# Stick-breaking running products: read from PSUM, written to one row of all keys

## The chip, the core and the metric

One core of a Trainium2 chip runs the whole program. A core has five engines that work at the same time, each through its own queue in order: TensorE (PE, matrix products; its weight loads are shown as PEld), VectorE (DVE), ScalarE (ACT), GpSimd (POOL) and SyncE (SP), which issues the DMA transfers. Data lie in SBUF (on-chip memory) or in PSUM (eight banks of 512 float32 columns over 128 partitions, into which TensorE writes its sums). The metric is the device time of one execution in microseconds; the figure given is the median of several runs.

## The reference

Two decoder layers on an input of 2048 positions by 1024 channels, float32. Layer 0 has four forgetting-attention heads ("f") and four stick-breaking heads ("s") of width 128, layer 1 has dilated-window heads. The change touches the stick-breaking heads alone. With z the scaled scores of a query t against the keys s < t:

```python
log_beta = jax.nn.log_sigmoid(z)
log_one_minus = jnp.where(strict, log_beta - z, 0.0)
...
w = jnp.where(strict, jnp.exp(log_beta + later), 0.0)   # later: sum of log_one_minus over the keys after s, before t
outs.append(jnp.einsum('bhqk,bhkd->bhqd', w.astype(v.dtype), v[:, :, :end]))
```

So a weight is sigmoid(z) at its key, times the product of sigmoid(-z) over all later keys of that query: a running product from the last key backwards.

## The kernel before

The program runs in stages: the projection of layer 0 (to about 745 us of the profiled execution), attention of layer 0 (`even_attention`: forgetting heads to about 1003 us, stick-breaking heads to about 1363 us), then layer 1. Every float32 product is made of three passes over high and low halves (`mm3`, lines 91 to 93); a `split` makes the halves, the high one on ACT (line 81), the low one by a subtraction on DVE (line 86).

`even_attention` works in units (kind, head, u): 256 queries, as two blocks i of 128, against all keys up to them. There are 8 units per head and 64 in all. For each block, `qk` goes over the keys in chunks of 512 columns from the last chunk to the first. Per chunk of a stick-breaking head:

- TensorE puts scores into a PSUM bank `ps` (lines 91 to 93; in the last chunk a mask is added, line 733);
- ACT writes sigmoid(-z) to `omb`, a 512-column SBUF buffer out of a ring of four (line 744), and sigmoid(z) into the unit's tile `rows` (line 745);
- DVE scans `omb` backwards in place (line 747): a running product whose start is `carry`, the first column of the scan of the chunk before (that is, of the later keys);
- GpSimd multiplies `rows` with the running product, shifted by one column (line 749, n - 1 columns);
- DVE multiplies the last column of the chunk, whose factor lies in the buffer of the chunk before, with `carry` (line 751, one column).

That is 160 chunks, of which 96 have a `carry`. `pv` then takes the finished `rows` of a unit: TensorE transposes them (line 783), ACT and DVE split them into `pT`, and TensorE multiplies with the values into one bank `po`; DVE multiplies the sum with the gate (line 801). `merged` interleaves `qk` of unit n with `pv` of unit n - 2.

Names and buffers: `k.ps("s")` has four PSUM banks, shared by the scores and `po`; `k.ps("t")` has four more, for the transposes. `k.big` gives one of eight large SBUF slots; during attention each resident head takes two (`kt`, `vt`), the next head's two are taken from u = 4 on, and each unit in flight has one for `rows`. The `res` ring of `k.c2` (four) holds `omb`.

Which instruction stands where in an engine's queue is decided when the program is built: a planner places the instructions by the order of the program text and an estimate of their durations, gives them slots, and adds the waits that data and slots need.

Of the kernel before, what the change touches and what calls it, by code (L numbers as in the profile page):

```python
# [11 lines left out]
AF = mybir.ActivationFunctionType  # L12
OP = mybir.AluOpType
# [4 lines left out]
P = 128  # L18
S = 2048
D = 1024  # L20
KT = D // P
CH = 512
# [14 lines left out]
class K:  # L37
# [28 lines left out]
    def c2(self, shape=(P, CH), dt=F32, name="c2", tag="c"):  # L66

        return self.cs.tile(list(shape), dt, name=name, tag=tag, bufs={"c": 4, "res": 4}.get(tag, 2))
# [608 lines left out]
def merged(*gens):  # L677

    live = [[g, n, 0] for g, n in gens]
    while live:  # L680
        live.sort(key=lambda e: (e[2] + 0.5) / e[1])
        e = live[0]
        if next(e[0], "end") == "end":
            live.remove(e)
        e[2] += 1
# [3 lines left out]
def even_attention(k, tail):  # L689
    tc, nc = k.tc, k.nc  # L690
    c2 = k.c2
    scale = float(P) ** -0.5
    heads, bias = {}, {}

    def load_head(kind, h):
        T, V = (k.fT, k.v["f"]) if kind == "f" else (k.sT, k.v["s"])
        kt = k.big([P, 4, 2, CH], F32R, name="kt")
        vt = k.big([P, 4, 2, TPC, P], F32R, name="vt")

        def chunk(c):  # L700
            s = slice(c * CH, (c + 1) * CH)
            nc.sync.dma_start(kt[:, c].bitcast(F32), T["k"][:, h, :, s].bitcast(F32))
            for z in range(2):
                nc.sync.dma_start(vt[:, c, z].bitcast(F32),
                                  V[s, z, h * P:(h + 1) * P].rearrange("(j p) d -> p j d", p=P).bitcast(F32))

        heads[kind, h] = kt, vt
        return chunk

    def load_q(kind, h, u):  # L710
        T = k.fT if kind == "f" else k.sT
        if kind == "f" and u % 2 == 0:
            c = u // 2
            bias[h, c] = c2(name="bias")
            nc.sync.dma_start(bias[h, c], k.ncum[h:h + 1, c * CH:(c + 1) * CH].to_broadcast([P, CH]))
        q = c2([P, 2, 2 * P], F32R, name="qT", tag="q")
        nc.sync.dma_start(q.bitcast(F32), T["q"][:, h, :, u * 2 * P:(u + 1) * 2 * P].bitcast(F32))
        return q

    def qk(kind, h, u, q, tile):  # L720
        kt, vt = heads[kind, h]
        c = u // 2
        for i in range(2):
            rows = tile[:, i]
            a = [q[:, z, i * P:(i + 1) * P] for z in range(2)]
            nk = (u * 2 + i + 1) * P
            carry = None
            for kc in range(c, -1, -1):
                n = CH if kc < c else nk - c * CH
                ps = k.ps("s")  # L730
                k.mm3(ps[:, :n], a, [kt[:, kc, z, :n] for z in range(2)], True, kc < c)
                if kc == c:
                    nc.tensor.matmul(ps[:, n - P:n], k.identb, k.after if kind == "f" else k.notbefore,
                                     start=False, stop=True)
                dst = rows[:, kc * CH:kc * CH + n]
                if kind == "f":
                    m = k.small.tile([P, 1], F32, name="m")
                    nc.vector.tensor_tensor_reduce(
                        out=dst, in0=ps[:, :n], in1=bias[h, kc][:, :n], op0=OP.add, op1=OP.max,
                        scale=1.0, scalar=3.0 * NEG if carry is None else carry, accum_out=m)  # L740
                    carry = m
                else:
                    o = c2(name="omb", tag="res")
                    nc.scalar.activation(o[:, :n], ps[:, :n], AF.Sigmoid, scale=-scale)  # L744
                    nc.scalar.activation(dst, ps[:, :n], AF.Sigmoid, scale=scale)
                    oo = o[:, :n]
                    nc.vector.tensor_tensor_scan(oo[:, ::-1], oo[:, ::-1], oo[:, ::-1],  # L747
                                                 1.0 if carry is None else carry, OP.mult, OP.bypass)
                    nc.gpsimd.tensor_tensor(dst[:, :n - 1], dst[:, :n - 1], o[:, 1:n], op=OP.mult)  # L749
                    if carry is not None:  # L750
                        nc.vector.tensor_tensor(dst[:, n - 1:n], dst[:, n - 1:n], carry, op=OP.mult)  # L751
                    carry = o[:, 0:1]
                yield
            if kind == "f":
                nm = k.small.tile([P, 1], F32, name="nm")
                nc.vector.tensor_scalar(nm, carry, -1.0, None, op0=OP.mult)
                den = k.small.tile([P, 2], F32, name="den")
                cuts = [(b, min(b + 2 * CH, nk)) for b in range(0, nk, 2 * CH)]
                for z, (b, e) in enumerate(cuts):
                    nc.scalar.activation(rows[:, b:e], rows[:, b:e], AF.Exp, bias=nm,  # L760
                                         accum_out=den[:, z:z + 1])
                if len(cuts) == 2:
                    nc.vector.tensor_tensor(den[:, :1], den[:, :1], den[:, 1:], op=OP.add)
                rd = k.small.tile([P, 1], F32, name="rd")
                nc.vector.reciprocal(rd, den[:, :1])
                for b, e in cuts:
                    nc.gpsimd.tensor_scalar(rows[:, b:e], rows[:, b:e], rd, 1.0, op0=OP.mult, op1=OP.mult)

    def pv(kind, h, u, rows):

        vt = heads[kind, h][1]
        po = k.ps("s")
        gt = c2([P, 2 * P], name="gate", tag="pT")
        m = (0 if kind == "f" else 4) + h
        cols = slice(u * 2 * P, (u + 1) * 2 * P)
        nc.sync.dma_start(gt, k.gT[:, m, cols])

        def transposed(jj):
            pt = k.ps("t")
            hl = k.wps.tile([P, 2, 2, 2 * P], F32R, name="pT", tag="wp")  # L780
            for jx in range(2):
                for i in range(jx if jj == u else 0, 2):
                    nc.tensor.transpose(pt[:, (jx * 2 + i) * P:(jx * 2 + i + 1) * P],  # L783
                                        rows[:, i, (jj * 2 + jx) * P:(jj * 2 + jx + 1) * P], k.ident)
            flat = [hl[:, z].rearrange("p j t -> p (j t)") for z in range(2)]
            for s in (slice(0, 2 * P), slice(3 * P, 4 * P)) if jj == u else (slice(0, 4 * P),):
                k.split(flat[0][:, s], flat[1][:, s], pt[:, s])
            return hl

        ready = transposed(0)  # L790
        for jj in range(u + 1):
            yield
            hl = ready
            if jj < u:
                ready = transposed(jj + 1)
            for jx in range(2):
                j = jj * 2 + jx
                i0 = P if jj == u and jx else 0
                a = [vt[:, j // TPC, z, j % TPC] for z in range(2)]
                k.mm3(po[:, i0:2 * P], a, [hl[:, z, jx, i0:] for z in range(2)], j == 0, j == 2 * u + 1)  # L800
        nc.vector.tensor_tensor(gt, po[:, :2 * P], gt, op=OP.mult)
        nc.sync.dma_start(k.mixT[:, m, cols], gt)
# [4 lines left out]
    def slopes(g, hf):  # L807

        t = k.w4([P, HG, 2, P], name="slopes")
        for h in range(HG):  # L810
            slope = 2.0 ** (-8.0 * (g * HEADS + hf * HG + h + 1) / (3 * HEADS))
            nc.gpsimd.tensor_scalar(t[:, h], k.dist, -slope32(slope) * GROUPS[g][1], 1.0, op0=OP.mult, op1=OP.mult)
        nc.sync.dma_start(k.bias[g, hf], t)
# [6 lines left out]
    q = load_q(*units[0])  # L820
# [2 lines left out]
    past = []  # L823
    for n, (kind, h, u) in enumerate(units):
        rows = k.big([P, 2, S], name="rows")
        gens = [(qk(kind, h, u, q, rows), 2 * (u // 2 + 1))]
        if n + 1 < len(units):
            q = load_q(*units[n + 1])
        nxt = order.index((kind, h)) + 1
        if u == 1 and nxt <= 6:  # L830
            slopes((nxt - 1) // 2, (nxt - 1) % 2)
        if nxt < len(order) and u >= 3:
            if u == 3:
                chunk = load_head(*order[nxt])
            else:
                chunk(u - 4)
        if len(past) == 2:
            v = past.pop(0)
            gens.append((pv(*v[0], v[1]), v[0][2] + 1))
        merged(*gens)  # L840
        past.append(((kind, h, u), rows))
# [389 lines left out]
```

## Time and profile before

| | |
|---|---|
| median of 3 runs | 2896.94 us (2895.7 to 2902.72) |
| the profiled execution | 2898.2 us, its span 2896.1 us |
| TensorE, weight loads | 93%, 85% of the span busy |
| VectorE | 73% |
| ScalarE | 57% |
| GpSimd | 44% |
| mean granted TensorE clock | 0.975 of full speed |

The profile is a record of one execution. A group of instructions is shown as: line, engine, operation, output<-inputs, shape, xcount | busy us, mean ns of one | idle time of the engine just before them and what ended it. A row of waits is: who waited <- for whom: us in total, times, longest. A row of the timeline is: start in us, duration in us, engine, line, operation. Busy shares in the slices are tenths (9 is 90% or more), 40 slices over the span, each 72.4 us.

### The profile page before, as it was taken

How to read it: one execution, taken by the hardware profiler on the slowest of the kernel's cores; microseconds unless marked ns; L12 is line 12 of the kernel's file. 1: busy time of each engine (PE TensorE's matmuls, PEld its weight loads, DVE VectorE, ACT ScalarE, POOL GpSimd, SP SyncE). 2: the span in 40 equal slices, each digit the busy share in tenths (PEclk: the TensorE clock that was granted, in tenths of full speed). 3: DMA queues.
4: the chain of work that ended last, by engine and by line, in shares of the span. 5: the costliest groups of instructions: out<-in, count | busy, mean ns of one | idle time of the engine just before them, and what ended most of it. 6: DMA issues, size and time to landing. Idle time of an engine off the chain costs nothing.

```text
span 2896.1 us, 56017 instructions
## 1 busy us (share of the span) xinstructions
PE 2693.4 (93%) x20191; PEld 2467.0 (85%) x20191; DVE 2107.1 (73%) x4480; ACT 1650.2 (57%) x3992; POOL 1281.4 (44%) x996
## 2 busy tenths in 40 slices
PE   4999999999999988887887999999989999999998
PEld 3899878998899877776887999999978999999876
DVE  7747785675677799999976966666687586663866
ACT  5446453465566666665455564555565477765642
POOL 5545365434233355555654745343335442422322
PEclk8999999999999999998998999999999999999999
DMA  3556635545544433312567463424533445444665
GB/s 117 168 170 224 197 125 170 168 129 185 159 152 135 137 106 116 110 48 75 177 204 228 147 215 99 145 94 148 163 123 98 139 147 161 139 139 138 217 233 197
DMA packets 388164, 437.39 MB, mean 151 GB/s; under 512 B 31472, under 2 KB 319536, under 8 KB 387888
## 3 DMA queue, kind: packets, MB, share of 16 engines
q1 hardware_dynamic: 387888, 433.83, 46.4%
q8 instruction: 159, 2.61, 0.4%
q14 instruction: 117, 0.96, 0.1%
HBM read 279.16 MB, written 154.57 MB: 150 GB/s over the span
## 4 chain that ended last, share of the span: by engine, by line
PE 61%; DVE 24%; DMA 5%; issue 4%; ACT 4%; POOL 1%; SPq 1%; DVEq 0%; ACTq 0%; POOLq 0%
PE ps L91 16%; PE ps L92 16%; PE ps L93 16%; DVE omb L747 4%; PE ps L783 3%; DVE A L86 2%; DVE wop L86 2%; PE ps L1035 2%; DVE S L86 2%; PE ps L1025 2%; PE ps L1006 2%; PE ps L951 1%; DVE lp L319 1%; DVE pT L86 1%; DVE c L277 1%
## 5 line engine op out<-in xcount | busy, mean ns | idle before, releaser
L210 POOL TENSOR_TENSOR wraw<-wraw 128x512 f32<-128x512 f32 (+1 forms) x320 | 444.4, 1396 | 486.5 <-DVE wop L86 210.8
L81 ACT ACTIVATE wop<-wraw 128x512 fp32r<-128x512 f32 (+1 forms) x560 | 350.6, 630 | 372.0 <-PE ps L93 302.1
L86 POOL TENSOR_TENSOR wop<-wraw,wop 128x512 fp32r<-128x512 f32 (+1 forms) x240 | 328.7, 1372 | 508.7 <-ACT wop L81 490.4
L91 PE MATMUL ps<-wop,S 128*128 128x256 f32 (+1 forms) x1792 | 518.9, 290 | 20.0 <-DVE c L277 10.2
L92 PE MATMUL ps<-wop,S 128*128 128x256 f32 (+1 forms) x1792 | 514.2, 287 | 12.2 <-DVE wop L86 9.4
L92 PE MATMUL ps<-wop,A 128*128 128x256 f32 (+1 forms) x1792 | 512.4, 286 | 6.2 <-DVE wop L86 6.0
L91 PE MATMUL ps<-wop,A 128*128 128x256 f32 (+1 forms) x1792 | 511.8, 286 | 6.8 <-ACT u L282 3.1
L93 PE MATMUL ps<-wop,S 128*128 128x256 f32 (+1 forms) x1792 | 514.8, 288 | 0.0
L93 PE MATMUL ps<-wop,A 128*128 128x256 f32 (+1 forms) x1792 | 509.7, 285 | 0.0
L86 DVE TENSOR_TENSOR wop<-wraw,wop 128x512 fp32r<-128x512 f32 (+1 forms) x320 | 266.8, 835 | 236.1 <-ACT wop L81 234.8
L91 PEld LDWEIGHTS ps<-wop,S 128*128 128x128 f32 x1792 | 343.6, 192 | 25.6 <-ACT wop L81 9.6
L92 PEld LDWEIGHTS ps<-wop,S 128*128 128x128 f32 x1792 | 344.4, 192 | 15.4 <-DVE wop L86 10.3
L91 PEld LDWEIGHTS ps<-wop,A 128*128 128x128 f32 x1792 | 341.8, 191 | 11.3 <-issue 4.0
L92 PEld LDWEIGHTS ps<-wop,A 128*128 128x128 f32 x1792 | 342.5, 191 | 8.7 <-DVE wop L86 7.6
L93 PEld LDWEIGHTS ps<-wop,S 128*128 128x128 f32 x1792 | 344.4, 192 | 3.6 <-issue 2.9
L93 PEld LDWEIGHTS ps<-wop,A 128*128 128x128 f32 x1792 | 342.6, 191 | 1.4 <-issue 0.9
L749 POOL TENSOR_TENSOR rows<-rows,omb 128x511 f32<-128x511 f32 (+3 forms) x160 | 189.9, 1198 | 162.4 <-DVE rows L751 76.5
L81 ACT ACTIVATE pT<-ps 128x512 fp32r<-128x512 f32 (+2 forms) x352 | 166.9, 508 | 137.0 <-PE ps L783 69.2
L277 DVE TENSOR_TENSOR c<-u,ps 128x512 f32<-128x512 f32 (+1 forms) x254 | 165.2, 657 | 98.3 <-PE ps L93 86.6
L747 DVE TENSOR_TENSOR_SCAN omb<-omb 128x512 f32<-128x512 f32 (+3 forms) x160 | 220.0, 1379 | 5.9 <-ACT omb L744 3.4
L86 DVE TENSOR_TENSOR pT<-ps,pT 128x512 fp32r<-128x512 f32 (+2 forms) x352 | 189.3, 560 | 31.2 <-ACT pT L81 30.0
L92 PE MATMUL ps<-pT,vt 128*128 128x256 f32 (+1 forms) x576 | 182.2, 317 | 30.7 <-DVE pT L86 30.5
(216 smaller groups left out, 6619.3 us busy)
## 6 DMA issues: line engine op xcount, KB each, us to landing
wraw<-in_odd_w_in_dram SPq DMA_DIRECT2D x80, 512.0 KB, 3.9
wraw<-in_even_w_in_dram SPq DMA_DIRECT2D x64, 512.0 KB, 4.4
ld<-qk SPq DMA_DIRECT2D x106, 256.0 KB, 3.1
qk<-c SPq DMA_DIRECT2D x96, 256.0 KB, 2.4
lp<-hT SPq DMA_DIRECT2D x60, 256.0 KB, 3.4
uu<-ot SPq DMA_DIRECT2D x96, 132.0 KB, 2.0
fin<-uu SPq DMA_DIRECT2D x16, 792.0 KB, 4.8
hT<-te SPq DMA_DIRECT2D x48, 256.0 KB, 3.9
```

Source lines behind the costliest of these rows:

```text
L81: nc.scalar.activation(hi, src, AF.Copy)
L86: (nc.vector if lo_on == "dve" else nc.gpsimd).tensor_tensor(lo, src, hi.bitcast(F32), op=OP.subtract)
L91: mm(out, a[0], b[0], start=start, stop=False, skip_group_check=more)
L92: mm(out, a[0], b[1], start=False, stop=False, skip_group_check=more)
L93: mm(out, a[1], b[0], start=False, stop=stop, skip_group_check=more)
L210: tt = lambda e, o, x, y, op, s: e.tensor_tensor(o[:, s], x[:, s], y[:, s], op=op)
L277: nc.vector.tensor_tensor(out[g], x[g], y[g], op=OP.add)
L747: nc.vector.tensor_tensor_scan(oo[:, ::-1], oo[:, ::-1], oo[:, ::-1], 1.0 if carry is None else carry, OP.mult, OP.bypass)
L749: nc.gpsimd.tensor_tensor(dst[:, :n - 1], dst[:, :n - 1], o[:, 1:n], op=OP.mult)
L783: nc.tensor.transpose(pt[:, (jx * 2 + i) * P:(jx * 2 + i + 1) * P], rows[:, i, (jj * 2 + jx) * P:(jj * 2 + jx + 1) * P], k.ident)
L1006: nc.tensor.matmul(scores(hp, e), q[pr, za, hp], ring[pr, zb, hp, blocks], start=i == 0, stop=i == 2)
L1025: nc.tensor.transpose(pp[:, i * P:(i + 1) * P], row[:, h // 2, h % 2, b], k.ident)
```

## The change

In `qk`, for stick-breaking heads: each unit gets a second large slot, `rest`, of the same shape as `rows`, passed as `left`. ACT writes sigmoid(z) to `rows` first and then sigmoid(-z) over the scores in their PSUM bank. The scan reads that bank backwards and writes to the columns of the chunk in `rest`; its second operand, which the operation bypasses, is one column of the identity matrix, repeated. Since the running products of all chunks now lie side by side, the GpSimd product of a chunk with a later neighbour covers all n columns, the shifted operand reaching one column into that neighbour, and the one-column product on DVE is gone. The buffer `omb` is gone too.

```diff
-    def qk(kind, h, u, q, tile):
+    def qk(kind, h, u, q, tile, left):
...
+                b = kc * CH
...
-                dst = rows[:, kc * CH:kc * CH + n]
+                dst = rows[:, b:b + n]
...
-                    o = c2(name="omb", tag="res")
-                    nc.scalar.activation(o[:, :n], ps[:, :n], AF.Sigmoid, scale=-scale)
                     nc.scalar.activation(dst, ps[:, :n], AF.Sigmoid, scale=scale)
-                    oo = o[:, :n]
-                    nc.vector.tensor_tensor_scan(oo[:, ::-1], oo[:, ::-1], oo[:, ::-1],
+                    nc.scalar.activation(ps[:, :n], ps[:, :n], AF.Sigmoid, scale=-scale)
+                    o = left[:, i]
+                    back = ps[:, :n][:, ::-1]
+                    nc.vector.tensor_tensor_scan(o[:, b:b + n][:, ::-1], back, k.ident[:, :1].to_broadcast([P, n]),
                                                  1.0 if carry is None else carry, OP.mult, OP.bypass)
-                    nc.gpsimd.tensor_tensor(dst[:, :n - 1], dst[:, :n - 1], o[:, 1:n], op=OP.mult)
-                    if carry is not None:
-                        nc.vector.tensor_tensor(dst[:, n - 1:n], dst[:, n - 1:n], carry, op=OP.mult)
-                    carry = o[:, 0:1]
+                    w = n - 1 if carry is None else n
+                    nc.gpsimd.tensor_tensor(dst[:, :w], dst[:, :w], o[:, b + 1:b + 1 + w], op=OP.mult)
+                    carry = o[:, b:b + 1]
...
         rows = k.big([P, 2, S], name="rows")
-        gens = [(qk(kind, h, u, q, rows), 2 * (u // 2 + 1))]
+        rest = k.big([P, 2, S], name="rest") if kind == "s" else None
+        gens = [(qk(kind, h, u, q, rows, rest), 2 * (u // 2 + 1))]
```

## The prediction

> **What bounds it now.** I read the page first: engine shares, the slices, the groups.
>
> ```profile
> PE 2693.4 (93%) x20191; PEld 2467.0 (85%) x20191; DVE 2107.1 (73%) x4480; ACT 1650.2 (57%) x3992; POOL 1281.4 (44%) x996
> PE   4999999999999988887887999999989999999998
> DVE  7747785675677799999976966666687586663866
> ```
>
> Over the span TensorE is the bound. Not so in slices 15 to 19, where VectorE (DVE) stands at 9 and PE drops to 7 or 8. That is the stick-breaking stage, about 1003 to 1363 us. I then took the windows view of it and of 200 us of the forgetting stage before it, which has the same tiling.
>
> ```profile
> core 0: us, PE busy (x) PEld busy (x) DVE busy (x) ACT busy (x) POOL busy (x), PEclk, DMA share, GB/s
> 800.00:900.00 100.00, 99.53 (x741) 91.18 (x740) 77.31 (x252) 60.63 (x137) 28.88 (x34) 1.00 0.48 150
> 900.00:1000.00 100.00, 99.93 (x722) 90.70 (x721) 82.03 (x263) 63.16 (x139) 33.24 (x38) 1.00 0.44 136
> 1003.00:1363.00 360.00, 302.63 (x1969) 264.71 (x1970) 339.51 (x484) 230.10 (x513) 196.87 (x166) 0.93 0.29 90
> ```
>
> With DVE 79.7% busy (159.3 of 200 us) PE idles 0.3%. With DVE 94.3% busy (339.5 of 360) PE idles 15.9%, or 57.4 us. The chain of waits cut to this window and the waits view say who is late:
>
> ```profile
> by line: DVE omb L747 36.0%; issue 11.8%; DVE pT L86 9.4%; PE ps L92 7.8%; PE ps L93 6.8%; PE ps L91 6.7%; PE ps L783 6.4%; DVE rows L751 2.1%; ACT omb L744 2.1%; DVE gate L801 1.9%; DVE A L86 1.6%; DMA vt<-sv 1.4%; DMA gate<-gT 1.4%; ACT p
> ...
> PEld ps L92 <- DVE pT L86: 36.9, 25, 4.6
> PE ps L92 <- DVE pT L86: 30.5, 22, 4.1
> ...
> PE ps L91 <- DVE gate L801: 14.3, 9, 2.6
> ...
> DVE omb L747 <- ACT omb L744: 3.4, 9, 0.8
> ```
>
> PE waits for the low halves (L86) and gate products (L801) that queue on DVE behind the scans (L747). The scans themselves almost never wait. So here DVE work is time. Its groups, by form:
>
> ```profile
> L747 DVE TENSOR_TENSOR_SCAN omb<-omb 128x512 f32<-128x512 f32 x112 | 180.0, 1609 | 5.0 <-ACT omb L744 2.6
> L86 DVE TENSOR_TENSOR pT<-ps,pT 128x512 fp32r<-128x512 f32 x115 | 75.3, 677 | 12.4 <-ACT pT L81 12.3
> L751 DVE TENSOR_TENSOR rows<-rows,omb 128x1 f32<-128x1 f32 x96 | 26.2, 273 | 0.0
> L747 DVE TENSOR_TENSOR_SCAN omb<-omb 128x384 f32<-128x384 f32 x16 | 16.1, 1004 | 0.1
> L747 DVE TENSOR_TENSOR_SCAN omb<-omb 128x256 f32<-128x256 f32 x16 | 15.1, 943 | 0.0
> L747 DVE TENSOR_TENSOR_SCAN omb<-omb 128x128 f32<-128x128 f32 x16 | 9.3, 583 | 0.8 <-ACT omb L744 0.8
> ```
>
> Why does a 512-wide scan take 1609 ns? The timeline shows single ones:
>
> ```profile
> 1055.73 1.27 DVE L747 TENSOR_TENSOR_SCAN omb<-omb 128x512 f32<-128x512 f32 x1
> 1056.92 0.13 DVE L751 TENSOR_TENSOR rows<-rows,omb 128x1 f32<-128x1 f32 x1
> 1056.97 0.68 DVE L86 TENSOR_TENSOR pT<-ps,pT 128x512 fp32r<-128x512 f32 x1
> ...
> 1062.67 2.21 DVE L747 TENSOR_TENSOR_SCAN omb<-omb 128x512 f32<-128x512 f32 x1
> 1062.72 1.09 POOL L749 TENSOR_TENSOR rows<-rows,omb 128x511 f32<-128x511 f32 x1 [1.57 <-ACT rows L745]
> ...
> 1064.86 0.68 DVE L747 TENSOR_TENSOR_SCAN omb<-omb 128x256 f32<-128x256 f32 x1
> ...
> 1304.40 0.94 DVE L747 TENSOR_TENSOR_SCAN omb<-omb 128x384 f32<-128x384 f32 x1
> ```
>
> Alone it takes 1.27 us; beside a GpSimd product of 1.09 us it takes 2.21, nearly the sum. The two exclude each other, and since each product starts as its scan ends, it meets the next scan. Which DVE instructions suffer? The view of line 86 and of tile omb, durations as minimum/median/maximum:
>
> ```profile
> L86 DVE TENSOR_TENSOR pT<-ps,pT x180: 257/674/693, 1002.7 to 1362.4; 128x512 fp32r<-128x512 f32 x115, 128x256 fp32r<-128x256 f32 x33, 128x128 fp32r<-128x128 f32 x32
> L86 DVE TENSOR_TENSOR A<-stage,A x8: 674/680/1769, 1341.5 to 1352.7; 128x512 fp32r<-128x512 f32 x8
> ...
> L747 DVE TENSOR_TENSOR_SCAN omb<-omb x160: 407/1283/2305, 1004.2 to 1360.0; 128x512 f32<-128x512 f32 x112, 128x128 f32<-128x128 f32 x16, 128x256 f32<-128x256 f32 x16, 128x384 f32<-128x384 f32 x16
> L751 DVE TENSOR_TENSOR rows<-rows,omb x96: 125/128/1150, 1018.0 to 1361.2; 128x1 f32<-128x1 f32 x96
> ```
>
> The same subtraction never exceeds 693 ns in 180 cases when one input is in PSUM, and reaches 1769 when both are in SBUF. Scan and one-column product have both inputs in SBUF today.
>
> **The change, part by part.**
>
> One-column products: 96 go. They are busy 26.2 us, but a free one ends almost wholly under its successor (0.13 long, the next starts 0.05 after it), so 0.08 each comes off: 26.2 - 96 x 0.08 = 18.5 us of DVE occupancy. Their work moves into the GpSimd product, one column wider (512 for 511), 1 part in 500: nothing, GpSimd being 55% busy.
>
> Scan input from PSUM. The new scan has one PSUM stream and one SBUF column read again and again. Its form is not in the trace, so bounds: by the pT row (one PSUM, one SBUF input) it loses the collisions; by its own row of today it keeps 1609. I take the first, since the operands are of the kinds in the pT row. Then 112 x (1.609 - 1.27) = 38.0, and for the small forms 16 x (1.004 - 0.94), 16 x (0.943 - 0.68) and 16 x (0.583 - 0.407) = 1.0 + 4.2 + 2.8. Sum 46.0 us. Dearer PSUM reads: 674 ns with PSUM against 680 without, nothing.
>
> [...]
>
> Sigmoids: two per chunk as before (L744, L745), but the row's comes first and the scan now waits for both, 0.62 us later per chunk at the start of a run of chunks. DVE's queue covers it (its whole wait on L744 is 3.4 us). ACT, 64% busy, writes as many elements to PSUM instead of SBUF: nothing.
>
> Banks. The score bank was free after the second sigmoid; now it is held through the scan. Four banks of this kind, one taken by pv's sum, so three chunks in flight; the four-deep ring of omb goes. The nearest row is the forgetting stage, where DVE also hands back all 160 score banks:
>
> ```profile
> L91 PEld LDWEIGHTS ps<-kt,qT 128*128 128x128 f32 x320 | 62.9, 197 | 12.4 <-DVE gate L801 4.9 <-DVE m L738 4.2
> L744 ACT ACTIVATE omb<-ps 128x512 f32<-128x512 f32 x112 | 69.4, 619 | 48.0 <-PE ps L93 24.3 <-DVE rows L751 18.8 <-PE ps L733 1.6
> L745 ACT ACTIVATE rows<-ps 128x512 f32<-128x512 f32 x112 | 69.7, 622 | 0.0
> ...
> L91 PE MATMUL ps<-kt,qT 128*128 128x512 f32 x112 | 51.2, 457 | 2.7 <-DVE gate L801 2.7
> L92 PE MATMUL ps<-kt,qT 128*128 128x512 f32 x112 | 44.9, 401 | 0.0
> L93 PE MATMUL ps<-kt,qT 128*128 128x512 f32 x112 | 44.8, 400 | 0.0
> ```
>
> PE's weight loads waited 4.2 us for L738 there: the low end, at least 0. The high end is the wait on gate today, 14.3 us for 32 banks, 0.45 each, so 72 us for 160. I take 5, near the first, because DVE will be loaded as in that stage rather than as today.
>
> Large slots. Eight; each stick-breaking unit now takes two (rows, rest). With two heads' keys and values resident, three units' rows and one rest, all eight are full, where one was spare. That holds at 12 unit borders (into units 4 to 7 of three heads): the next rest waits for the last product, at most 1.09 us plus the 0.13 us of a handover, about 15 us in all. In the gap DVE has low halves of pv to do, 0.68 us each; I take 3. pv and the product of the next unit would queue behind a scan that waits there. DMA issues: none added; those of the next head are not moved.
>
> Sum. DVE's occupancy becomes 339.5 - 18.5 - 46.0 = 275.0 us. PE's idle share between the two stages of the windows view runs from 0.3% at 79.7% DVE to 15.9% at 94.3%, so 1.07 points per point. The length T that fits is 323 us: DVE 85.1%, idle 0.3 + 1.07 x 5.4 = 6.1%, 302.6 / 0.939 = 322. Gain 37, less 5 and 3: 29. The profiled execution took 2898.2 (span 2896.1 and 2.1 around it), 1.3 above the median of 2896.9; the gain is taken off the median: 2868. What is late next is PE, then DVE's low halves.
>
> **Rivals.**
>
> Bank hold (the other side). A bank's turn needs 0.457 + 0.401 + 0.400 of matmuls, 0.619 + 0.622 of sigmoids and 1.27 of scan, 3.77 us; three banks give a chunk per (3.77 + queueing) / 3. Today's pace is 360 / 160 = 2.25 us, so it decides at 2.98 us of queueing per turn; at 4 us the pace is 2.59, the stage 414 us, the kernel 2951. For it: DVE's queue is deep and PE and ACT serve pv too. Against: 4.2 us in the forgetting stage.
>
> The collisions stay, because the broadcast column comes from SBUF. Then DVE is 321 us, T by the same line 350, gain 10, less 8: 2895, no change. For it: the second operand is in SBUF. Against: so is that of the pT row.
>
> More gain: PE's stalls vanish and its clock (0.93 here, 1.00 before) recovers. DVE at today's 94.3% then bounds: 275 / 0.943 = 292, gain 68: 2829. Against: PE still depends on DVE and ACT in every pv step.
>
> The scan is ordered behind the product of the chunk before, as both touch tile rest though not the same columns: 1.27 + 1.09 and two handovers of 0.13, 2.62 per chunk, 419 us, 2956. Against: today a sigmoid writes one part of rows while a product works on another.
>
> **How the numbers follow.** Forecast 63% (2868, its own range 2850 to 2885), more gain 10%, collisions stay 8%, bank hold 15% (a third of it near no change, the rest slower), ordering 4%. Change under 0.3% (8.7 us) can't be told from none. So faster 0.73, same 0.08 + 0.05 = 0.13, slower 0.10 + 0.04 = 0.14. The range 2838 to 2905 leaves out half of "more gain" and most of what is slower, under 2 in 10.
>
> **What would show it.** Right: scans of 512 at 1.27 to 1.35 us with a maximum near the median; no one-column group; about 275 us of DVE and 6% of PE idle in a stage of some 330 us; products at 1.09 with fewer above. Wrong: a scan mean still near 1.6 (collisions stay); PE or its weight loads waiting on the scan for tens of us (bank hold); scans waiting on GpSimd (slots, ordering); a longer time elsewhere, since the planner lays the whole program out anew.

## The result and the profile after

The changed kernel takes 2847.2 us (median of 4 runs, 2843.92 to 2850.04) against 2897.57 us for the kernel before (4 runs, 2895.7 to 2902.72). The ratio is 0.9823, 95% interval 0.9806 to 0.984: 1.8% faster, about 50 us. A later measurement of both gave 2849.76 and a ratio of 0.9836 (0.9814 to 0.9859). The forecast was 2868, range 2838 to 2905.

The page after, shares and two rows of the slices:

```profile
PE 2678.1 (94%) x20191; PEld 2452.8 (86%) x20191; DVE 2051.4 (72%) x4384; ACT 1649.6 (58%) x3992; POOL 1247.2 (44%) x996
PE   4999999999999999998887999999989999999998
DVE  7747885566588788888957857566697586763876
```

DVE has 96 instructions fewer. In the slices of the stage, 15 to 19, it is at 8 where it was at 9, and PE is at 9 up to slice 18. The stage itself, in the windows view, each time up to about 3 us after the last scan of the stick-breaking heads began (1360.0 before, 1313.2 after; the row of before stands in the prediction):

```profile
1003.00:1316.20 313.20, 287.13 (x1964) 249.03 (x1962) 276.30 (x386) 227.43 (x512) 157.59 (x164) 0.97 0.34 104
```

The stage is 46.8 us shorter, nearly the whole gain. DVE's occupancy fell from 339.5 to 276.3 us, PE's from 302.6 to 287.1, and the clock granted to PE rose from 0.93 to 0.97. PE now idles 8.3% of it. The DVE groups by form in the stage, and for the scans with a `carry` the minimum/median/maximum from the view of tile rest:

```profile
L750 DVE TENSOR_TENSOR_SCAN rest<-ps,rest,ident 128x512 f32<-128x512 f32 x96 | 122.7, 1279 | 16.8 <-ACT ps L747 12.9
L750 DVE TENSOR_TENSOR_SCAN rest<-ps,ident 128x512 f32<-128x512 f32 x16 | 19.3, 1206 | 0.0
L750 DVE TENSOR_TENSOR_SCAN rest<-ps,ident 128x384 f32<-128x384 f32 x16 | 15.0, 940 | 2.6 <-ACT ps L747 2.1 <-PE ps L735 0.5
L750 DVE TENSOR_TENSOR_SCAN rest<-ps,ident 128x256 f32<-128x256 f32 x16 | 10.9, 682 | 2.0 <-ACT ps L747 1.9
L750 DVE TENSOR_TENSOR_SCAN rest<-ps,ident 128x128 f32<-128x128 f32 x16 | 6.5, 404 | 1.0 <-ACT ps L747 1.0
```

```profile
L750 DVE TENSOR_TENSOR_SCAN rest<-ps,rest,ident x96: 1267/1282/1286, 1016.2 to 1313.2; 128x512 f32<-128x512 f32 x96
```

Every scan takes what a free one took before (1.27 us): none of 96 exceeds 1286 ns, where the mean was 1609 and the longest 2305. It is not that GpSimd keeps away. The timeline shows a product and a scan that start together and do not delay each other:

```profile
1100.55 1.09 POOL L753 TENSOR_TENSOR rows<-rows,rest 128x512 f32<-128x512 f32 x1 [0.65 <-DVE rest L750]
1100.57 1.21 DVE L750 TENSOR_TENSOR_SCAN rest<-ps,ident 128x512 f32<-128x512 f32 x1
```

Nor does a scan wait for the product of the chunk before it. Here three scans with a `carry`, of consecutive chunks of one block, follow each other with some 0.1 us between (4.04 us in all for three of 1.27 to 1.28), while the products of the first two run beside the second and the third:

```profile
1059.44 4.04 DVE L750 TENSOR_TENSOR_SCAN rest<-ps,rest,ident 128x512 f32<-128x512 f32 x3
1060.79 1.09 POOL L753 TENSOR_TENSOR rows<-rows,rest 128x512 f32<-128x512 f32 x1 [2.78 <-DVE rest L750]
1062.18 1.09 POOL L753 TENSOR_TENSOR rows<-rows,rest 128x512 f32<-128x512 f32 x1 [0.30 <-DVE rest L750]
```

The chain of waits in the stage, and the waits of PE:

```profile
by line: DVE rest L750 21.0%; PE ps L91 9.7%; PE ps L92 9.7%; PE ps L93 9.2%; DVE pT L86 9.1%; PE ps L785 8.0%; issue 7.9%; ACT rows L746 4.8%; DMA gate<-gT 4.6%; ACT ps L747 4.4%; ACT pT L81 3.7%; DMA mixT<-gate 2.3%; DVE A L86 2.0%; DVE g
```

```profile
PEld ps L91 <- DVE rest L750: 25.9, 36, 2.1
...
DVE rest L750 <- ACT ps L747: 17.8, 25, 1.7
...
PE ps L91 <- DVE rest L750: 13.8, 24, 2.0
...
PEld ps L92 <- DVE pT L86: 7.2, 8, 3.0
```

The scans' share of the chain fell from 36.0% to 21.0%. PE's weight loads wait 7.2 us for low halves (36.9 before), but a new wait has come: 25.9 and 13.8 us (the same stalls in part, seen by loads and by matmuls) for a scan to give back its score bank. And scans now wait 17.8 us for the second sigmoid, 3.4 before.

### The profile page after: what moved, and what is told of

It is laid out like the page before. It is cut to its first block, busy times and chain, and to the rows that moved or that the text cites. A ratio compares the mean times of both kernels' runs of the same rounds, so it can differ in the third digit from the quotient of the medians.

```text
span 2846.3 us, 55611 instructions
## 1 busy us (share of the span) xinstructions
PE 2678.1 (94%) x20191; PEld 2452.8 (86%) x20191; DVE 2051.4 (72%) x4384; ACT 1649.6 (58%) x3992; POOL 1247.2 (44%) x996
## 4 chain that ended last, share of the span: by engine, by line
PE 46%; DVE 16%; DMA 6%; ACT 4%; issue 3%; POOL 1%; SPq 0%; DVEq 0%; ACTq 0%; POOLq 0%
PE ps L91 12%; PE ps L92 12%; PE ps L93 12%; PE ps L785 3%; DVE rest L750 2%; PE ps L1038 2%; PE ps L1028 2%; DVE wop L86 2%; PE ps L1009 1%; DVE S L86 1%; PE ps L954 1%; DVE A L86 1%; DVE pT L86 1%; DVE lp L319 1%; DMA fin<-uu 1%
## 5 line engine op out<-in xcount | busy, mean ns | idle before, releaser
L753 POOL TENSOR_TENSOR rows<-rows,rest 128x512 f32<-128x512 f32 (+4 forms) x160 | 153.3, 966 | 153.1 <-DVE rest L750 147.3
L1021 ACT ACTIVATE row<-row,nm 128x256 f32<-128x256 f32 (+1 forms) x384 | 172.4, 451 | 59.1 <-DVE nm L1019 58.6
```

What stands on the lines that cost most here:

```text
L753: nc.gpsimd.tensor_tensor(dst[:, :w], dst[:, :w], o[:, b + 1:b + 1 + w], op=OP.mult)
L1021: nc.scalar.activation(row[:, h // 2, h % 2, :nk], row[:, h // 2, h % 2, :nk], AF.Exp, bias=nm[:, h:h + 1], accum_out=ot[:, HW + HG + h:HW ...
```

## The experiments

**Each part alone.** The row without PSUM (the edits of this section are shown shortened; `scan` stands for `nc.vector.tensor_tensor_scan`):

```diff
-  nc.scalar.activation(dst, ps[:, :n], AF.Sigmoid, scale=scale)
-  nc.scalar.activation(ps[:, :n], ps[:, :n], AF.Sigmoid, scale=-scale)
-  back = ps[:, :n][:, ::-1]
-  scan(o[:, b:b + n][:, ::-1], back, ident column, ...)
+  nc.scalar.activation(o[:, b:b + n], ps[:, :n], AF.Sigmoid, scale=-scale)
+  nc.scalar.activation(dst, ps[:, :n], AF.Sigmoid, scale=scale)
+  back = o[:, b:b + n][:, ::-1]
+  scan(back, back, back, ...)
```

> The contiguous row and the wide product alone: the scan works in place in the row, both of its inputs in SBUF, and the score bank is free after the sigmoids. Theory (the gain is mostly that the scan, with one input in PSUM, no longer excludes the GpSimd product): scans of 512 stay near 1.6 us with maxima above 2.2; DVE loses only the one-column products, 18 us; time 2880 to 2890, stage about 347 us, TensorE clock there about 0.93 to 0.95. Rival (the gain is the one-column products and the chain over chunk borders that they made): time within 8 us of 2847.

Measured 2887.85 us, ratio 0.9971 (0.9959 to 0.9982). Its groups, its scans as minimum/median/maximum in a second profile, and its stage:

```profile
L750 DVE TENSOR_TENSOR_SCAN rest<-rest 128x512 f32<-128x512 f32 x112 | 179.5, 1608 | 5.4 <-ACT rest L747 2.4
```

```profile
1003.00:1338.50 335.50, 289.06 (x1953) 248.65 (x1952) 321.80 (x384) 226.24 (x508) 203.75 (x163) 0.97 0.32 96
```

```profile
L750 DVE TENSOR_TENSOR_SCAN rest<-rest x160: 412/1314/2301, 1001.7 to 1336.7; 128x512 f32<-128x512 f32 x112, 128x128 f32<-128x128 f32 x16, 128x256 f32<-128x256 f32 x16, 128x384 f32<-128x384 f32 x16
```

The collisions are all there, and DVE lost 17.7 us, as the theory priced the one-column products (18.5). So the rival that these are the gain falls. The time lies in the band expected (2880 to 2890), but not for the reason: the stage was 24.5 us shorter (expected 347, measured 335.5) at a clock of 0.97 (expected 0.93 to 0.95), and 14 of the 24.5 us are gone again by the end.

Why the stage gained more than the 17.7 us of DVE was not tested. One wait may bear on it: in the kernel before, ACT waits 22.0 us for one-column products to give back a buffer of the `omb` ring (18.8 of them stand in the row of L744 in the prediction). With the row this wait is gone.

PSUM without the row (the kernel before, with the scan reading the score bank):

```diff
-  nc.scalar.activation(o[:, :n], ps[:, :n], AF.Sigmoid, scale=-scale)
   nc.scalar.activation(dst, ps[:, :n], AF.Sigmoid, scale=scale)
+  nc.scalar.activation(ps[:, :n], ps[:, :n], AF.Sigmoid, scale=-scale)
-  scan(oo[:, ::-1], oo[:, ::-1], oo[:, ::-1], ...)
+  scan(oo[:, ::-1], ps[:, :n][:, ::-1], ident column, ...)
```

> The kernel before with one edit: sigmoid(-z) goes over the scores in PSUM and the scan reads it there, writing omb as before; the one-column products stay. Theory: scans of 512 at 1.27 to 1.29 us, one-column products still up to 1.1 us beside a GpSimd product; DVE occupancy of the stage about 293 us, stage about 326 us, time about 2860. Rival (one-column products): time within 9 us of 2897.

Measured 2879.73 us, ratio 0.9947 (0.9928 to 0.9967): a miss by 20 us. Groups, stage and two instructions of its timeline:

```profile
L747 DVE TENSOR_TENSOR_SCAN omb<-ps,omb,ident 128x512 f32<-128x512 f32 x96 | 122.4, 1275 | 6.4 <-ACT ps L745 4.4
L751 DVE TENSOR_TENSOR rows<-rows,omb 128x1 f32<-128x1 f32 x96 | 41.6, 434 | 7.0 <-ACT rows L744 4.3
```

```profile
1003.00:1347.00 344.00, 297.64 (x1974) 253.10 (x1975) 311.20 (x484) 229.56 (x514) 160.31 (x167) 0.97 0.31 95
```

```profile
1059.40 1.09 POOL L749 TENSOR_TENSOR rows<-rows,omb 128x511 f32<-128x511 f32 x1 [1.97 <-DVE omb L747]
1059.42 1.08 DVE L751 TENSOR_TENSOR rows<-rows,omb 128x1 f32<-128x1 f32 x1
```

The scans are free, but the next DVE instruction with two SBUF inputs, the one-column product, now meets the GpSimd product and waits it out: 1.08 us for one column, 434 ns on average where it was 273. So DVE stands at 311 and not at 293. That is not the whole of the miss: PE's weight loads also wait 41.0 us here for a scan to give back its score bank, more than in the changed kernel (25.9).

Neither part does alone what both do: DVE falls by 17.7 with the row, by 28.3 with PSUM, by 63.2 with both. Moving the one-column products off DVE, still without the row, tests that:

```diff
-  nc.vector.tensor_tensor(dst[:, n - 1:n], dst[:, n - 1:n], carry, op=OP.mult)
+  nc.gpsimd.tensor_tensor(dst[:, n - 1:n], dst[:, n - 1:n], carry, op=OP.mult)
```

> The scan from PSUM into omb as in the run with the one-column products (2880), but these 96 products run on GpSimd; there is no contiguous row. Theory (the one-column products cost what they hold of DVE, more so when they meet the GpSimd products): DVE occupancy of the stage 276 to 282 us, stage 312 to 325 us, time 2846 to 2860. Rival (the contiguous row itself, by dropping the ring of four omb buffers that wait for the one-column products, is what gains): DVE falls, but the stage stays above 335 us and the time above 2870.

```profile
1003.00:1317.90 314.90, 283.77 (x1965) 245.22 (x1965) 278.43 (x387) 226.34 (x510) 174.20 (x261) 0.99 0.33 103
```

Measured 2857.97 us, ratio 0.9874 (0.9857 to 0.9892). DVE is at 278, and the stage within 2 us of the changed kernel's. So, beside a scan from PSUM, the contiguous row gains by what it takes off DVE. The ring of omb buffers, still there, costs next to nothing in this form: one scan waits 1.0 us for it. (ACT does not write `omb` here, so this says nothing of its 22.0 us in the kernel before.) Most of the 11 us to the changed kernel came after the stage: the last scan began 1.7 us later (1314.9), the last issue of tile gg, near the end of the program, 5.6 us later (2709.6 against 2704.0), and from there to the end it took 5.5 us more.

**Which input, and who collides.** The scanned stream in SBUF again, only the second operand, which the operation ignores, from PSUM:

```diff
-  nc.scalar.activation(ps[:, :n], ps[:, :n], AF.Sigmoid, scale=-scale)
+  nc.scalar.activation(o[:, b:b + n], ps[:, :n], AF.Sigmoid, scale=-scale)
-  scan(o[:, b:b + n][:, ::-1], back, ident column, ...)
+  scan(back, back, ps[:, :n][:, ::-1], ...)              # back = o[:, b:b + n][:, ::-1]
```

> The changed kernel, but sigmoid(-z) is in the SBUF row and scanned there in place; the bypassed second operand is read from the score bank in PSUM instead. Theory (what counts is that only one input comes from SBUF, whichever): scans of 512 at 1.27 to 1.30 us, maxima near the median, time 2840 to 2855. Rival (the scanned stream itself has to come from PSUM): scans near 1.6 us, time 2880 to 2890.

```profile
L750 DVE TENSOR_TENSOR_SCAN rest<-rest,ps x160: 392/1270/1282, 1003.0 to 1310.3; 128x512 f32<-128x512 f32 x112, 128x128 f32<-128x128 f32 x16, 128x256 f32<-128x256 f32 x16, 128x384 f32<-128x384 f32 x16
```

Measured 2852.4 us, ratio 0.9848 (0.9826 to 0.987), scans at most 1282 ns. Reading the data from PSUM is not what helps. What helps is that only one of the two inputs comes from SBUF (1282 ns at most, against 2301 with both from SBUF); the ignored operand counts like the data.

Without the GpSimd product (the line is deleted from the kernel before):

> The kernel before without the GpSimd product of line 749, so the weights of these heads lack the running product in all but the last columns of chunks. Theory (the product is what the scan and the one-column product wait for): scans of 512 at 1.27 to 1.28 us, one-column products at 0.13, DVE occupancy about 270 to 277 us, time 2840 to 2855. Rival (a scan in place with two SBUF streams is slow by itself, or slowed by DMA or ACT): scans near 1.6 us, time above 2885.

```profile
L747 DVE TENSOR_TENSOR_SCAN omb<-omb 128x512 f32<-128x512 f32 x112 | 143.6, 1283 | 6.6 <-ACT omb L744 2.8 <-ACT rows L745 0.5
...
L750 DVE TENSOR_TENSOR rows<-rows,omb 128x1 f32<-128x1 f32 x96 | 12.8, 134 | 0.0
```

```profile
1284.23 1.66 POOL L210 TENSOR_TENSOR wraw<-wraw 128x512 f32<-128x512 f32 x1 [281.57 <-DVE wop L86]
...
1284.66 2.30 DVE L747 TENSOR_TENSOR_SCAN omb<-omb 128x512 f32<-128x512 f32 x1
```

Measured 2839.49 us, ratio 0.9803 (0.9788 to 0.9819), a little faster than expected, with 279.3 us of DVE in the stage (270 to 277 expected). With both inputs in SBUF the scans are free (1283 ns in the mean) once GpSimd is nearly idle, 5.6 us busy in the stage. A scan of 2.30 us is left: it meets one of the three GpSimd instructions that the stage still has. That closes the case for the collision: removing either partner frees the scan.

**The bank hold.** pv's sum moved to the transposes' banks (`po = k.ps("t")`), so that scores have four:

> The changed kernel with the sum of pv in a bank of the transposes' four, so that the scores have four banks instead of three. Theory: holding the score bank through the scan costs PE part of its waits on the scan (25.9 us of weight loads, 13.8 of matmuls); with a fourth bank those fall below half, but the transposes lose one of four and PE waits more on the low halves; net between 2838 and 2852. Rival (the bank hold is covered): the waits fall and the time stays within 4 us of the changed kernel run beside it.

```profile
800.00:900.00 100.00, 95.03 (x688) 87.76 (x687) 69.10 (x217) 55.65 (x118) 26.01 (x31) 0.97 0.35 108
900.00:1000.00 100.00, 94.17 (x671) 85.67 (x669) 76.20 (x247) 58.27 (x129) 27.29 (x32) 0.98 0.51 154
```

```profile
PEld ps L91 <- DVE rest L750: 25.3, 50, 1.3
...
PE ps L91 <- DVE rest L750: 14.6, 37, 1.1
```

Measured 2885.01 us, ratio 0.9968 (0.9955 to 0.9982): both views missed. (The profile is of the slowest of its ten executions, 2894.37.) The waits on the scan did not fall. `pv` serves the forgetting heads too, so this edit reaches their stage as well, and PE is only 94 to 95% busy there, where the changed kernel has 99.8%. The transposes have one bank less; that this is the cause was not tested. Better was to let scores of every other chunk, of all heads, use the transposes' banks:

```diff
-  ps = k.ps("s")
+  ps = k.ps("s" if kc % 2 else "t")
```

> The changed kernel with the scores of every other chunk in a bank of the transposes' four, so that scores and transposes share all eight. Theory of the bank hold: PE's waits on the scan fall, time 2835 to 2850. Rival: transposes queue behind banks that wait for the scan, PE waits on DVE rise, time above 2855.

```profile
1003.00:1303.20 300.20, 274.87 (x1912) 241.15 (x1911) 270.23 (x375) 226.44 (x500) 156.35 (x161) 0.98 0.35 106
```

```profile
PEld ps L91 <- DVE rest L750: 6.0, 9, 1.1
```

Measured 2846.82 us, ratio 0.983 (0.9802 to 0.9857). The weight loads' waits for score banks fell from 25.9 us (23.8 in the second profile below) to 6.0, and the last scan began 13 us (10) earlier. Part of this came from the forgetting heads, which the edit also touches: the first scan began 3 to 4 us earlier. From first to last scan the stage took 300.4 us, against 309.7 and 308.0. Nor is it free, since transposes now share banks with scores: the weight loads wait 19.1 us for low halves (7.2 in the changed kernel), and transposes wait for scans (6.6 us at PE). So the bank hold is real, and giving scores more banks gains, net, some 8 us of the stage. But the time beside it is 2849.76, with overlapping intervals: at the first issue of tile x1d, some 50 us after the last scan, 4.5 of the 10 us were left (1356.1 against 1360.6). For stick-breaking heads alone:

> The changed kernel with the scores of every other chunk in a bank of the transposes' four, for stick-breaking heads alone. Theory of the bank hold: PE's waits on the scan fall from 24 and 14 us to under 10 each and the stage shortens by 8 to 13 us, as when all heads alternated; the next stage takes part of that back, time 2838 to 2847. Rival (what follows sets the end whatever the stage does): stage shorter, time within 3 us of the changed kernel's 2847 to 2850.

Measured 2857.24 us, ratio 0.987 (0.9852 to 0.9887), with the waits at 7.4 us and the last scan at 1307.1: some 8 us more than the changed kernel, a miss of both views. The scans took 303.3 us from first to last, so the stage still gained; of the loss, some 5 us lie behind the last issue of gg (151.0 us to the end, 146.4 in the second profile of the changed kernel). No version tried is clearly faster than the changed kernel with the computation whole.

**Is the clock a matter of chance?** Both kernels once more, unchanged:

> The changed kernel once more, beside the others. Theory (the granted clock of the stage follows from how often PE stalls in this kernel): stage clock 0.96 to 0.99, PE busy in the stage 284 to 290 us, time 2844 to 2852. Rival (the clock of the stage differs from run to run by chance): clock below 0.95 and PE busy above 295.

> The kernel before once more, for a second profile. Theory (clock follows the stalls): stage clock 0.91 to 0.95 and PE busy 298 to 306 us of some 360. Rival (chance): clock 0.97 or more and PE busy below 292 in a stage of the same length.

```profile
1003.00:1313.70 310.70, 284.11 (x1960) 245.71 (x1959) 276.17 (x386) 226.68 (x509) 157.10 (x163) 0.99 0.34 104
```

```profile
1003.00:1361.80 358.80, 302.23 (x1969) 263.31 (x1970) 339.75 (x484) 229.90 (x513) 196.28 (x166) 0.93 0.30 91
```

First after, then before. Clock and PE busy time come out as in the first profiles: they belong to the kernels. In the traces of the two kernels the granted clock is either 1.00 or 0.50. In the stage of the kernel before, eleven stretches at 0.50 fill 53.7 us (51.9 in the second profile); in the changed kernel four fill 17.8 us (three fill 9.1). In the timeline before, matmuls of the same form follow each other every 0.12 us at full clock (1279.77 to 1280.25, four steps) and every 0.215 us at half (1293.42 to 1294.28), so 0.44 of a half-clock stretch is lost. Of the difference of 35.9 us (42.8) that makes 16 us (19), an estimate; PE's busy time fell by 15.5 (18.1). With PSUM alone this does not come out: 23.9 us at half clock, but PE busy 297.6 us; why stays open.

What comes ahead of such a stretch is seen in the kernel before, in windows of 2 us (columns as above, PE first, PEclk third from the end):

```profile
1288.50:1290.50 2.00, 1.40 (x7) 0.78 (x5) 1.89 (x2) 1.99 (x6) 0.78 (x2) 1.00 0.54 178
1290.50:1292.50 2.00, 0.00 (x0) 0.00 (x0) 2.00 (x4) 0.33 (x1) 0.78 (x2) 0.94 0.00 0
1292.50:1294.50 2.00, 1.96 (x8) 1.74 (x9) 1.89 (x5) 1.03 (x3) 0.82 (x2) 0.50 0.21 70
1294.50:1296.50 2.00, 2.00 (x11) 1.91 (x11) 2.00 (x3) 0.72 (x3) 2.00 (x2) 0.50 0.03 4
1296.50:1298.50 2.00, 2.00 (x12) 2.00 (x11) 2.00 (x4) 1.05 (x2) 0.78 (x2) 0.50 0.22 66
```

PE stands still for 2.64 us behind a gate product on DVE (1289.90 to 1292.54), and from 1292.3 it has half its clock for 6.8 us. So this stall cost more than its length. The half-clock stretches that lie wholly in the two stages last 3.41 or 6.83 us. Each of the eleven in the stage of the kernel before has, in the 5 us ahead of it, a time of 1.1 to 4.1 us without matmuls. But behind three such times of 2.21, 2.55 and 2.32 us (from 1038.15, 1051.78 and 1335.47) the clock stayed at 1.00, so the length of one stall does not tell what follows; what decides it was not shown.

**Where the lost 14 us of the row in SBUF went.** The same kernel again:

> The run with the row in SBUF once more, for a second profile: its stage was 24 us shorter than before and its time only 8. Theory (its last part is laid out otherwise by the planner and is slower each time): last stick-breaking scan near 1335 us, and from the last issue of gg to the end again 154 to 160 us, against 146 before. Rival (that profile caught a late transfer by chance): 143 to 149 us, and a span near 2875.

Span 2881.9, last scan at 1336.7. Of the 14 us, 3 were lost between the stage and the last issue of gg. From there to the end it took 150.4 us (2731.5 to 2881.9), in the first profile 157.6 (2728.4 to 2886.0), before 146.1 (2750.0 to 2896.1) and after 142.3 (2704.0 to 2846.3). The second profiles of the last two have 143.5 and 146.4, so this part differs by 3 to 7 us between two profiles of each of the three kernels. Neither expectation held; the last part is slower than before in both profiles, by 4 and 11 us. The order of its instructions is another in each kernel, because the planner lays out everything anew; whether that is the cause was not shown.

## Why the prediction was right, and where its size was off

Sign, place and the mechanism on DVE were right, and the range held; the likeliest case's own range (2850 to 2885) missed by 3 us. Step by step:

- One-column products 18.5 us of DVE: 17.7 with the row alone.
- Collisions 46.0 us: DVE fell by 63.2 in all, which leaves 45 to 46 beside the products; with the one-column products still there PSUM gave only 28.3. Taking the pT row's price for the new form was right (1282 ns against 1.27 us).
- DVE occupancy of the stage 275.0: measured 276.3. Reads from PSUM were put at no more than those from SBUF, and none dearer by more than some 12 ns was seen: the scans of 512 take 1206 ns without a `carry` and 1282 with one (median), against 1.27 us for a free one in SBUF.
- PE's idle share by the line through two stages: at the measured DVE share of 88.2% the line gives 9.4%, measured 8.3%. As a general law it is poor: without the product DVE stood at 92.5% (279.3 of 301.8 us), where the line gives 14.0% and 7.8% was measured.
- **The term that failed is PE's work, 302.6 us taken as fixed in "302.6 / 0.939 = 322".** It was 287.1, and the time at half clock accounts for it: 53.7 us before, 17.8 after. With 287.1 the same working gives a stage of 314, not 322. The forecast had the clock's recovery as a rival ("more gain", 10%), not as a part of the forecast, though the row with 0.93 stood in front of it.
- The costs of 5 and 3 us were laid on top. The bank hold is there, some 8 us net by the alternating banks, but the line alone already gives more idle time (9.4%) than was measured with it (8.3%), so nothing had to be added. A wait of a scan for a large slot is not among the waits of the stage, in either profile. (The 0.13 us of a handover in that term stands in no row of the prediction. In the timeline before, a GpSimd product ends at 1069.33 and the weight load of a transpose that waited for it starts at 1069.46; a one-column product ends at 1064.94 and the GpSimd product that waited for it starts at 1065.03.)
- The second sigmoid was put at nothing, "DVE's queue covers it". It does not: scans waited 17.8 us for it, 3.4 before. What that costs of the stage was not measured.
- So the stage: forecast 322 + 8 = 330, measured 313.2. That is 17 of the 21 us by which 2868 missed 2847; the rest is within the scatter of the runs (2843.92 to 2850.04). Both errors, PE's work and the added costs, went the same way and did not cancel.
- The forecast lets the whole gain of the stage reach the end, and here it did (46.8 us of the stage, 49.8 of the span). That was partly luck: with the row alone 10 of 24.5 us reached the end in the first profile, with alternating banks 4 of 10.

Of the rivals, "the collisions stay" is refuted by the 1286 ns maximum, and "ordered behind the product" by the three scans that run through beside their products. The bank hold came: by the prediction's own sign, PE waiting on the scan "for tens of us", it showed itself (25.9 and 13.8 us), but far below the point at which it decides. The forecast of what is late next, "DVE's low halves", did not hold: PE's loads now wait longer for score banks (25.9 us) than for low halves (7.2).

## What to carry to other kernels

When an instruction's mean is far above its minimum, find what ran beside it on the other engines, and count the SBUF inputs: one input moved to PSUM freed 45 us of DVE here, and an operand that the operation ignores served as well as the data (1282 ns at most, against 1286). Look for all instructions of that kind: here, with the scans freed alone, the collision moved to the one-column products behind them, and the gain in DVE was 28 us. And when a stage's PE stalls go, take its work at the full clock, not at the busy time measured among them: here 302.6 x 0.93 = 281 us, an estimate, against 287.1 and 284.1 measured.

## What was not expected of the hardware

A one-column product can take as long as the GpSimd instruction that it meets (1.08 us beside 1.09). A constant column read again and again from SBUF beside a PSUM stream does not collide (1286 ns at most), while the same scan with both operands in SBUF does (up to 2301 ns). And after 2.64 us without PE work the granted clock was 0.50 for 6.8 us.
